# A hybrid decoder layer: query squares added in pairs of half-heads, queries split from an SBUF copy, keys transposed once, adding transfers in another order

## The chip, the core and the metric

The kernel runs on one NeuronCore of one Trainium2 chip. A core has a matrix engine (TensorE, here PE, with its weight loads shown as PEld), three elementwise engines (VectorE or DVE, ScalarE or ACT, GpSimd or POOL) and a queue engine (SyncE or SP). Each works through its own instruction list in order and waits on semaphores for the others. SBUF is the working memory of 128 partitions, PSUM the memory that PE writes. The metric is the device time of one execution in microseconds, as the median of several runs.

## The reference

The layer takes `x` of 512 tokens by 1024 channels in float32. Only the attention part is touched in what it computes; the MLP keeps its arithmetic.

```
u = rms_norm(x, norm_mix_g)                       # 512 x 1024
proj = u @ w_in                                   # queries, keys, values, GLU pair, two gates
q = rms_norm(q, q_norm_g) * HEAD_DIM ** -0.5      # 16 heads of 64
k = rms_norm(k, k_norm_g)                         # 4 heads of 64
attn = sliding_window_attention(q, k, v, sinks, rel_bias) @ w_attn_o   # blocks of 128, window 128
conv = conformer_conv(glu_in, ...)                # 31 taps per channel, layer norm, silu, projection
x = x + (sigmoid(gate_attn) * attn + sigmoid(gate_conv) * conv) @ w_out
x = x + square(relu(rms_norm(x, norm_mlp_g) @ w_ff1)) @ w_ff2          # 1024 -> 4096 -> 1024
```

`rms_norm` of the queries needs, for every token and head, the mean of 64 squares.

## The kernel before

**Precision.** PE multiplies in a reduced float32 form, `fp32r`. To keep float32 accuracy every operand is split into a high part (a cast to `fp32r`) and a low part (the value less its high part), and a product is three matmuls: high by high, high by low, low by high. A weight piece of 128x1024 therefore costs ACT a cast (`split_hi`, L469) and POOL a subtraction (`split_lo`, L474) before PE can use it. Transposes are matmuls against an identity.

**Order.** Nothing is scheduled automatically. The code registers closures with `at(position, function, ...)`; at the end they are sorted by position (L1536) and run, and each engine's list is what they issue in that order. In the first part one position is one step of a projection tile: six matmuls of 128x512 (two of the eight chunks of 128 channels, three products each), and a tile of 128 output columns is four steps. The tiles follow as `h0 h1 q0 h2 q1 h3 h4 h5 q2 h6 h7 q3`, where `h` is a pair of GLU tiles (gate `ps_g`, value `ps_a`) and `q` a query group of two tiles (`ps_q`), then the gates `ps_ta` and `ps_tc`. Between the steps stand the attention units, one for each of 4 groups g and 4 token blocks t, at 42 + 6 (4 g + t): scores (`sp`, L712 and L713), scale (L720, ACT), maximum (L727, DVE), exponentials (L735, ACT), division (L744, POOL), transpose of the probabilities (`ptp`, L752), their split (L755 ACT, L759 DVE) and the product with the values (`op`, L767 and L769). DVE runs the taps of the convolution (L826) through this whole stage, ACT and POOL a few of them (L817, L818).

**Keys.** The keys of all groups lie token by token in `kraw`. `k_hi` (ACT) and `k_lo` (POOL) write their high and low parts, each twice side by side so that both halves of the 128 partitions hold them; `k_stage` (L405) transposes both parts, four 128x128 blocks per part and group, and ACT copies each result out of PSUM (L409).

**Queries.** A query tile holds two heads of 64 rows. When PE has finished it, ACT takes the high part of each head from PSUM (`q_hi`, L547) and the squares of the whole tile (`q_square`, L550), and DVE the low part of each head (`q_lo`, L554). After a group's second tile ACT and POOL split all squares into high and low parts (L566, L569). At `QSUM` = 8.08 positions after the group, `q_sums` (L571) adds over the 64 rows on PE: for each of 2 tiles, 4 token blocks and 2 parts one matmul with the squares as weights and the two columns of `pair` as moving operand, 16 per group into `qms`. ACT adds epsilon (L578) and POOL takes the inverse root (L580), which scales the scores.

**MLP.** It is cut into four parts of 1024 hidden units, each with two phases (`w_ff1`, then `w_ff2`), and each phase is a product of 2x2 block matrices with seven products instead of eight, in Strassen's manner (numbers 1 to 7). A product takes 4 positions, half a weight block at a time: ACT makes the high piece (`pieceh`, L1168), DVE the low one (`piecel`, L1171), 24 or 48 matmuls use them. Sums of weight blocks are made by DVE (`block_sum`, L1161) or in flight: `fetch_add` (L1145) issues on POOL's queue a transfer that adds a block of HBM to one in SBUF. In the second phases the order is 1, 7, 6, 2, 5, 4, 3. The transfers that add for product 5 go into product 1's block once both its pieces are read, those for product 6 into product 7's block, those for product 4 into that block again after product 6. Each is issued 0.9 positions after its half's high piece.

Of the kernel before, what the change touches and what calls it, by code (L numbers as in the profile page):

```python
# [8 lines left out]
F32 = mybir.dt.float32  # L9
F32R = mybir.dt.float32r  # L10
# [7 lines left out]
P = 128  # L18
# [24 lines left out]
QSUM = 8.08  # L43
# [10 lines left out]
def tile_hybrid_block(  # L54
# [197 lines left out]
    pair = sm.tile([P, 16], F32R, name="pair", tag="ss16")[:, 0:2]  # L252
# [142 lines left out]
    def k_hi(j):  # L395
        if j == 0:
            k2["h"] = att.tile([P, 16, 2, HD], F32R, name="k2h", tag="qs")
            k2["l"] = gates[:, 0].rearrange("p k c -> p (k c)").rearrange("p (t a d) -> p t a d", a=2, d=HD)
        se.copy(k2["h"][:, :, j, :], k3)

    def k_lo(j):
        ge.tensor_tensor(out=k2["l"][:, :, j, :], in0=k3, in1=k2["h"][:, :, j, :].bitcast(F32), op=ALU.subtract)

    def k_stage(nm, dst, g):
        tp = ps1.tile([P, S], F32R, name=f"ktp_{nm}{g}", tag="tr")  # L405
        for t in range(NT):
            pe.transpose(tp[:, t * P:(t + 1) * P],
                         k2[nm][:, t * NG + g].rearrange("p a d -> p (a d)"), ident_r)
        se.copy(dst[:, g, :], tp.bitcast(F32))  # L409
# [4 lines left out]
    for j in range(2):  # L414
        at(4.5 + j, k_hi, j)
        at(6.5 + 2 * j, k_lo, j)
    for g in range(NG):
        at(9.5 + 2 * g, k_stage, "h", kTh, g)
        at(18.5 + 2 * g, k_stage, "l", kTl, g)
# [117 lines left out]
    def q_open(g):  # L537
        qTs[g] = qTt[:, (1 + g) % 2].rearrange("p k c -> p (k c)").rearrange("p (h t q) -> p h t q", t=NT, q=P)
        state["sq", g] = att.tile([P, 2, NT, P], F32, name=f"sq_{g}", tag="qs")

    def q_from(ps, a):
        rows = slice(a * HD, (a + 1) * HD)
        return rows, ps[rows].rearrange("p (t q) -> p t q", q=P)[:, :, ::-1]

    def q_hi(ps, g, j, a):
        rows, src = q_from(ps, a)
        se.copy(qTs[g][rows, 2 * j + a], src)  # L547

    def q_square(ps, g, j):
        se.activation(state["sq", g][:, j], ps.rearrange("p (t q) -> p t q", q=P)[:, :, ::-1], AF.Square)  # L550

    def q_lo(ps, g, j, a):
        rows, src = q_from(ps, a)
        ve.tensor_tensor(out=qTs[g][(1 - a) * HD:(2 - a) * HD, 2 * j + a], in0=src,  # L554
                         in1=qTs[g][rows, 2 * j + a].bitcast(F32), op=ALU.subtract)

    def pair_of():
# [1025 lines left out]
```

## Time and profile before

| what | value |
|---|---|
| median of 3 runs | 753.25 us (753.12 to 754.34) |
| profiled execution | 754.29 us, of which the profile's span 752.5 us |
| PE busy | 745.1 us, 99% of the span |
| DVE, ACT, POOL busy | 614.1, 463.8, 264.8 us |
| granted PE clock | 1.00 in every stage |
| bytes moved | 97.96 MB, 130 GB/s on average |

The stages by the profile's clock: keys and values of the input projection to 32 us, then the projection tiles with the attention units and the convolution to about 300 us, the three output projections to about 440 us, and the MLP to the end. A row of the groups reads: line, engine, operation, output <- inputs, shapes, count | busy us, mean ns of one | idle time of the engine just before, and what ended it. A row of the timeline reads: start us, duration us, engine, line, operation, and in square brackets the idle time before it with what ended it. Matmuls overlap in the pipeline, so the price of a matmul in a row of them is the distance between starts, not the duration. An f32 matmul that isn't a transpose appears as two rows.

### The profile page before, as it was taken

What the parts mean: (1) busy time and instruction counts of PE and PEld (TensorE: products, weight loads), DVE (VectorE), ACT (ScalarE), POOL (GpSimd) and SP (SyncE); (2) the same over time, 40 slices, a digit from 0 to 9 for tenths busy, and PEclk for the clock granted to TensorE, in tenths of its full rate; (3) what the DMA queues carried; (4) which work ended last, traced back from release to release, by engine and by line L of the source; (5) the groups of instructions that cost most, each with busy time, mean ns of one, the idle gap of its engine ahead of it and who ended that gap; (6) DMA issues with size and microseconds to landing.
All of it is one profiled execution on the core that took longest, in us unless ns stands there. A gap on an engine that the chain in (4) does not pass through costs nothing.

```text
span 752.5 us, 11081 instructions
## 1 busy us (share of the span) xinstructions
PE 745.1 (99%) x4146; PEld 644.7 (86%) x4146; DVE 614.1 (82%) x934; ACT 463.8 (62%) x755; POOL 264.8 (35%) x212
## 2 busy tenths in 40 slices
PE   9999999999999999999999999999999999999998
PEld 7888888888888888888888899879997899889976
DVE  7948988989988988878347679899779977998786
ACT  7647467868877766348225468763765467546752
POOL 0466777666676565433530002210121012101210
PEclk9999999999999999999999999999999999999999
DMA  8531122232114131613329107972697359834772
GB/s 320 197 104 37 56 73 96 85 112 84 57 59 139 56 112 57 223 57 112 112 71 345 35 26 144 247 197 85 155 220 191 106 132 230 196 116 122 171 156 112
DMA packets 64901, 97.96 MB, mean 130 GB/s; under 512 B 3104, under 2 KB 34384, under 8 KB 64848
## 3 DMA queue, kind: packets, MB, share of 16 engines
q1 hardware_dynamic: 55600, 79.44, 31.3%
q0 software_dynamic: 9248, 17.83, 13.5%
q8 instruction: 32, 0.52, 0.3%
q14 instruction: 21, 0.17, 0.1%
HBM read 95.13 MB, written 2.12 MB: 129 GB/s over the span
## 4 chain that ended last, share of the span: by engine, by line
PE 81%; DMA 6%; issue 5%; DVE 5%; ACT 2%; POOL 1%; DVEq 0%; POOLq 0%; ACTq 0%
PE ps_z L1205 9%; DMA block<-in_w_ff_dram 6%; PE ps_x L1200 5%; PE ps_y L1205 4%; PE ps_kv L1401 3%; PE ps_y L1200 3%; PE ps_x L1205 3%; PE ps_g L506 2%; PE ps_a L506 2%; PE ps_g L508 2%; PE ps_g L507 2%; PE ps_a L508 2%; PE ps_a L507 2%; PE ps_tc L508 2%; PE ps_tc L507 2%
## 5 line engine op out<-in xcount | busy, mean ns | idle before, releaser
L1168 ACT CAST pieceh<-block 128x1024 fp32r<-128x1024 f32 x112 | 115.8, 1049 | 76.7 <-DVE block L1161 22.9
L1171 DVE TENSOR_TENSOR piecel<-block,pieceh 128x1024 fp32r<-128x1024 f32 x112 | 135.6, 1219 | 28.5 <-ACT pieceh L1168 28.3
L826 DVE SCALAR_TENSOR_TENSOR cv<-h,wcol,cv 128x512 f32<-128x512 f32 x208 | 146.2, 746 | 0.7
L1147 POOL DMA_DIRECT2D block<-in_w_ff_dram x34 | 41.4, 1259 | 291.7 <-DVE piecel L1171 145.8
L1200 PE MATMUL ps_x<-xSh,pieceh 128*128 128x256 f32 x192 | 53.0, 276 | 0.0
L1200 PE MATMUL ps_x<-xSl,pieceh 128*128 128x256 f32 x192 | 53.0, 276 | 0.0
L1200 PE MATMUL ps_x<-xSh,piecel 128*128 128x256 f32 x192 | 53.0, 276 | 0.0
L1205 PE MATMUL ps_z<-piecel,aSh 128*128 128x512 f32 (+1 forms) x98 | 38.4, 392 | 1.5 <-DVE piecel L1171 1.5
L1205 PE MATMUL ps_z<-pieceh,aSh 128*128 128x512 f32 (+1 forms) x98 | 37.9, 386 | 0.5 <-ACT pieceh L1168 0.5
L1205 PE MATMUL ps_z<-pieceh,aSl 128*128 128x512 f32 (+1 forms) x98 | 37.7, 385 | 0.0
L1161 DVE TENSOR_TENSOR block<-block,block 128x1024 f32<-128x1024 f32 x30 | 36.5, 1221 | 0.8 <-DMA block<-in_w_ff_dram 0.4
L1200 PEld LDWEIGHTS ps_x<-xSh,pieceh 128*128 128x128 f32 x192 | 36.0, 188 | 0.0
L1200 PEld LDWEIGHTS ps_x<-xSl,pieceh 128*128 128x128 f32 x192 | 36.0, 188 | 0.0
L1200 PEld LDWEIGHTS ps_x<-xSh,piecel 128*128 128x128 f32 x192 | 36.0, 188 | 0.0
L735 ACT ACTIVATE s<-s,negm 128x257 f32<-128x257 f32 (+1 forms) x64 | 30.3, 477 | 7.2 <-DVE negm L727 7.0
L818 POOL TENSOR_TENSOR side<-side,tap 128x512 f32<-128x512 f32 x24 | 31.0, 1292 | 10.0 <-ACT tap L817 10.0
L1239 ACT CAST aSh<-c 128x1024 fp32r<-128x1024 f32 x16 | 16.8, 1053 | 23.5 <-DVE c L1253 11.1
L727 DVE CUSTOM_DVE_ANT_0 s<-sp,bias,vecs 128x256 f32<-128x256 f32 (+1 forms) x64 | 26.0, 445 | 6.4 <-ACT sp L720 6.1
L744 POOL TENSOR_TENSOR s<-s,r 128x1024 f32<-128x1024 f32 (+1 forms) x16 | 26.9, 1681 | 10.9 <-DVE r L739 10.8
L720 ACT ACTIVATE sp<-sp,y_q 128x256 f32<-128x256 f32 (+1 forms) x64 | 25.8, 420 | 7.0 <-PE sp L713 6.0
L474 POOL TENSOR_TENSOR wl_g<-raw_g,wh_g 128x1024 fp32r<-128x1024 f32 x8 | 19.3, 2409 | 30.3 <-ACT wh_g L469 30.3
L474 POOL TENSOR_TENSOR wl_wo<-raw_wo,wh_wo 128x1024 fp32r<-128x1024 f32 x8 | 19.8, 2480 | 25.2 <-ACT wh_wo L469 25.2
(335 smaller groups left out, 2495.2 us busy)
## 6 DMA issues: line engine op xcount, KB each, us to landing
block<-in_w_ff_dram SPq DMA_DIRECT2D x64, 512.0 KB, 5.9
block<-in_w_ff_dram POOLq DMA_DIRECT2D x34, 512.0 KB, 8.5
raw_g<-in_w_in_dram SPq DMA_DIRECT2D x8, 512.0 KB, 4.3
raw_a<-in_w_in_dram SPq DMA_DIRECT2D x8, 512.0 KB, 4.4
raw_q<-in_w_in_dram SPq DMA_DIRECT2D x8, 512.0 KB, 3.8
raw_ta<-in_w_in_dram SPq DMA_DIRECT2D x8, 512.0 KB, 3.8
raw_tc<-in_w_in_dram SPq DMA_DIRECT2D x8, 512.0 KB, 3.9
raw_wo<-in_w_attn_o_dram SPq DMA_DIRECT2D x8, 512.0 KB, 3.8
```

The costliest lines, as they stand in the source:

```text
L474: eng.tensor_tensor(out=lo, in0=raw, in1=hi.bitcast(F32), op=ALU.subtract)
L507: pe.matmul(ps, wh[:, k, :], al(k), start=False, stop=False)
L508: pe.matmul(ps, wl[:, k, :], ah(k), start=False, stop=(k == KD - 1))
L735: se.activation(s4[:, h, lo:2 * P + 1], s4[:, h, lo:2 * P + 1], AF.Exp, bias=negm[:, h:h + 1], scale=-1.0, accum_out=l4[:, h:h + 1])
L818: ge.tensor_tensor(out=side[ct], in0=side[ct], in1=tap, op=ALU.add)
L826: ve.scalar_tensor_tensor(out=cps[ct], in0=src, scalar=w, in1=cps[ct], op0=ALU.mult, op1=ALU.add)
L1147: ge.dma_start(tl["raw"][buf][:, ks, :], block(ph, i, j)[:, ks, :], accum_op=ALU.add)
L1161: ve.tensor_tensor(out=o, in0=a, in1=b, op=ALU.add)
L1168: se.copy(piece("h", n), tl["raw"][buf][:, 2 * h:2 * h + 2, :])
L1171: ve.tensor_tensor(out=piece("l", n), in0=tl["raw"][buf][:, 2 * h:2 * h + 2, :], in1=piece("h", n).bitcast(F32), op=ALU.subtract)
L1200: pe.matmul(o, b[:, c, w], a[:, k, :], start=(first and c + q + i == 0), stop=(k == 3 and i == 2), skip_group_check=True)
L1205: pe.matmul(acc[:, cols], a[:, k, w], b[:, c, cols], start=(first and c + i == 0), stop=(k == 3 and i == 2), skip_group_check=True)
```

## The change

It has four parts.

1. **Sums of squares.** The square of a tile is replaced by `q_square` per head and half-head: each call writes the squares of 32 rows to the 32 partitions of that head in one tile `sq`, first 32 channels in one half of it, last 32 in the other. POOL adds the two halves (`q_square_sum`, 128x512). `q_sums` is then one plain f32 matmul per token block, 4 per group, against `pick` with four columns. The split of the squares (L566, L569) and `pair` are gone. `QSUM` becomes 10.08 for the first two groups and 9.42 for the others.
2. **Queries.** DVE copies the finished tile from PSUM to `qraw` (`q_keep`); the high parts, the squares (ACT) and the low parts (now POOL) read that copy, at later positions (`HI`, `SQ`, `LO`).
3. **Keys.** ACT writes the keys themselves twice side by side in f32 (`k_twice`), PE transposes them once as f32, ACT casts the result to the high part, and DVE subtracts to the low part.
4. **Adding transfers.** In the MLP's second phases the two transfers into product 1's block move from about 5 and 3 positions before the phase to 1.0 and 1.05 after its start.

```diff
-QSUM = 8.08
+QSUM = (10.08, 10.08, 9.42, 9.42)
+HI, SQ, LO = (6.6, 4.6), (7.0, 8.6), (6.8, 4.8)
...
-    def k_hi(j):
...
-        se.copy(k2["h"][:, :, j, :], k3)
-    def k_lo(j):
-        ge.tensor_tensor(out=k2["l"][:, :, j, :], in0=k3, in1=k2["h"][:, :, j, :].bitcast(F32), op=ALU.subtract)
-    def k_stage(nm, dst, g):
...
+    def k_twice(j):
+        if j == 0:
+            k2["d"] = att.tile([P, 16, 2, HD], F32, name="k2d", tag="qs")
+        se.copy(k2["d"][:, :, j, :], k3)
+    def k_stage(g):
+        tp = k2["t", g] = ps1.tile([P, S], F32, name=f"ktp_{g}", tag="tr")
         for t in range(NT):
+            pe.transpose(tp[:, t * P:(t + 1) * P], k2["d"][:, t * NG + g].rearrange("p a d -> p (a d)"), ident)
+    def k_hi(g):
+        se.copy(kTh[:, g, :], k2["t", g])
+    def k_lo(g):
+        ve.tensor_tensor(out=kTl[:, g, :], in0=k2["t", g], in1=kTh[:, g, :].bitcast(F32), op=ALU.subtract)
...
     for g in range(NG):
-        at(9.5 + 2 * g, k_stage, "h", kTh, g)
-        at(18.5 + 2 * g, k_stage, "l", kTl, g)
+        at(9.5 + 2 * g, k_stage, g)
+        at(9.6 + 2 * g, k_hi, g)
+        at(9.8 + 2 * g, k_lo, g)
...
+    def q_keep(ps, g, j):
+        ve.tensor_copy(state["raw", g][:, j], ps.rearrange("p (t q) -> p t q", q=P)[:, :, ::-1])
+    def q_hi(g, j, a):
         rows = slice(a * HD, (a + 1) * HD)
+        se.copy(qTs[g][rows, 2 * j + a], state["raw", g][rows, j])
+    def q_square(g, j, a):
+        h = 2 * j + a
+        for half in range(2):
+            rows = slice(a * HD + 32 * half, a * HD + 32 * half + 32)
+            se.activation(state["sq", g][32 * h:32 * h + 32, half], state["raw", g][rows, j], AF.Square)
+    def q_lo(g, j, a):
+        rows = slice(a * HD, (a + 1) * HD)
+        ge.tensor_tensor(out=qTs[g][(1 - a) * HD:(2 - a) * HD, 2 * j + a], in0=state["raw", g][rows, j],
                          in1=qTs[g][rows, 2 * j + a].bitcast(F32), op=ALU.subtract)
...
+    def q_square_sum(g):
+        sq = state["sq", g]
+        ge.tensor_tensor(out=sq[:, 0], in0=sq[:, 0], in1=sq[:, 1], op=ALU.add)
     def q_sums(g):
...
-        for j in range(2):
-            for t in range(NT):
-                for n in "hl":
-                    pe.matmul(ms_ps[:, t, 2 * j:2 * j + 2], state["sq" + n, g][:, j, t, :], pair, start=n == "h", stop=n == "l")
+        for t in range(NT):
+            pe.matmul(ms_ps[:, t, :], state["sq", g][:, 0, t, :], pick, start=True, stop=True)
...
+            at(b + 4.2, lambda cell=cell, j=j: q_keep(cell["ps"], g, j))
             for a in range(2):
+                at(b + HI[j] + 0.1 * a, q_hi, g, j, a)
+                at(b + SQ[j] + 0.6 * a, q_square, g, j, a)
+                at(b + LO[j] + 0.4 * a, q_lo, g, j, a)
             b += 4
-        at(b + 0.9, q_square_hi, g)
-        at(b + 1.2, q_square_lo, g)
-        at(b + QSUM, q_sums, g)
-        at(b + QSUM + 0.4, q_root, g)
+        at(b + 6.6, q_square_sum, g)
+        at(b + QSUM[g], q_sums, g)
+        at(b + QSUM[g] + 0.4, q_root, g)
...
                 elif prod == 1:
-                    at(d, fetch_add, ph, h11, 0, 1, h)
+                    at(m + 1.0 + 0.05 * h, fetch_add, ph, h11, 0, 1, h)
```

Line numbers shift by three after the change, since it makes the file three lines shorter from the query part on.

Three places of the lists, of before and of the change. First, ACT at the third query group, around the second pair of exponentials (`s_...` with `negm`) of the attention unit next to the group's end; `h_...` with `cv` is a finished convolution tile, `tap` one of its taps, `wh_...` a high weight piece, `ms_q` the epsilon step after the sums. Before:

```order
L469 CAST wh_a_1_1636<-raw_a_1309 128x1024
L837 ACTIVATE h_782<-cv_927,wcol 128x512
L735 ACTIVATE s_1575,l_1577<-s_1575,negm_1576 128x257 x2
L817 ACTIVATE tap_3_1666<-h_1016,wcol 128x512
L703 COPY s_1684<-vecs 128x4
L578 ACTIVATE ms_q_1723<-qms_1706,eps_ln 128x16
```

and with the change:

```order
L470 CAST wh_a_1_1604<-raw_a_1276 128x1024
L834 ACTIVATE h_762<-cv_897,wcol 128x512
L732 ACTIVATE s_1543,l_1545<-s_1543,negm_1544 128x257 x2
L554 ACTIVATE sq_1438<-qraw_1437 32x512 x4
L814 ACTIVATE tap_3_1639<-h_990,wcol 128x512
L700 COPY s_1657<-vecs 128x4
```

The four squares of the group's second tile, which stood one piece ahead of `wh_g` as a single row of 128x512, now follow the exponentials, and the epsilon step has moved behind six more rows.

Second, POOL at the same group (`wl_...` a low weight piece, `s_...<-s_...,r_...` the division of the probabilities, `qTt` a low query part). Before:

```order
L474 TENSOR_TENSOR wl_g_1_1541<-raw_g_1180,wh_g_1_1540 128x1024
L569 TENSOR_TENSOR sql_1551<-sq_1470,sqh_1550 128x1024
L527 MEMSET h_1633 128x30
L474 TENSOR_TENSOR wl_a_1_1637<-raw_a_1309,wh_a_1_1636 128x1024
L744 TENSOR_TENSOR s_1575<-s_1575,r_1578 128x4x256
L818 TENSOR_TENSOR side_1192<-side_1192,tap_3_1666 128x512
```

and with the change:

```order
L475 TENSOR_TENSOR wl_g_1_1511<-raw_g_1147,wh_g_1_1510 128x1024
L558 TENSOR_TENSOR qTt<-qraw_1437,qTt 64x512 x2
L528 MEMSET h_1601 128x30
L475 TENSOR_TENSOR wl_a_1_1605<-raw_a_1276,wh_a_1_1604 128x1024
L741 TENSOR_TENSOR s_1543<-s_1543,r_1546 128x4x256
L568 TENSOR_TENSOR sq_1438<-sq_1438 128x512
L815 TENSOR_TENSOR side_1159<-side_1159,tap_3_1639 128x512
```

The low squares have gone, two low queries stand in their place, and the add of the two square halves stands behind the next low weight piece and a division.

Third, POOL's queue of transfers at the first two phases of the MLP: `block0` holds product 1's weights in the first second phase, `block3` product 7's. Before:

```order
L1147 DMA block1_3844<-in_w_ff1_dram 128x2x512 x2
L1147 DMA block3_3954<-in_w_ff2_dram 128x2x512 x2
L1147 DMA block0_3843<-in_w_ff2_dram 128x2x512 x2
L1147 DMA block3_3954<-in_w_ff2_dram 128x2x512 x4
L1147 DMA block1_3844<-in_w_ff2_dram 128x2x512 x2
```

and with the change:

```order
L1144 DMA block1_3799<-in_w_ff1_dram 128x2x512 x2
L1144 DMA block3_3909<-in_w_ff2_dram 128x2x512 x4
L1144 DMA block0_3798<-in_w_ff2_dram 128x2x512 x2
L1144 DMA block3_3909<-in_w_ff2_dram 128x2x512 x2
L1144 DMA block1_3799<-in_w_ff2_dram 128x2x512 x2
```

The two transfers into `block0` have moved behind the first two of the four into `block3`, those of product 7; the last two of the four, product 6's, stay behind both.

More of the change, by code (lines that the diff above doesn't have):

```diff
@@ L251, in tile_hybrid_block @@
     ssk = sm.tile([P, 16], F32, name="ssk", tag="ss16")
-    pair = sm.tile([P, 16], F32R, name="pair", tag="ss16")[:, 0:2]
+    pick = sm.tile([P, 16], F32, name="pick", tag="ss16")[:, 0:GRP]
     gates = gpool.tile([P, 2, KD, 256], F32R, name="gates", tag="gate")
@@ L414, in tile_hybrid_block @@
     for j in range(2):
-        at(4.5 + j, k_hi, j)
-        at(6.5 + 2 * j, k_lo, j)
+        at(4.5 + j, k_twice, j)
     for g in range(NG):
-        at(9.5 + 2 * g, k_stage, "h", kTh, g)
-        at(18.5 + 2 * g, k_stage, "l", kTl, g)
+        at(9.5 + 2 * g, k_stage, g)
+        at(9.6 + 2 * g, k_hi, g)
+        at(9.8 + 2 * g, k_lo, g)
     T_SHAPE = [P, KD, P]
@@ L538, in q_open @@
         qTs[g] = qTt[:, (1 + g) % 2].rearrange("p k c -> p (k c)").rearrange("p (h t q) -> p h t q", t=NT, q=P)
+        state["raw", g] = att.tile([P, 2, NT, P], F32, name=f"qraw_{g}", tag="qraw", bufs=2)
         state["sq", g] = att.tile([P, 2, NT, P], F32, name=f"sq_{g}", tag="qs")
-    def q_from(ps, a):
+    def q_keep(ps, g, j):
+        ve.tensor_copy(state["raw", g][:, j], ps.rearrange("p (t q) -> p t q", q=P)[:, :, ::-1])
+    def q_hi(g, j, a):
         rows = slice(a * HD, (a + 1) * HD)
-        return rows, ps[rows].rearrange("p (t q) -> p t q", q=P)[:, :, ::-1]
@@ L545, in q_hi @@
[L545 to L554, printed above, removed]
-                         in1=qTs[g][rows, 2 * j + a].bitcast(F32), op=ALU.subtract)
-    def pair_of():
-        low = eps_ln[:, 4:6]
-        ge.memset(low, 0.0)
-        for a in range(2):
-            ge.memset(low[a * HD:(a + 1) * HD, a:a + 1], 1.0 / HD)
-        ge.tensor_copy(pair, low)
@@ L564, in q_square_hi @@
-    def q_square_hi(g):
-        state["sqh", g], state["sql", g] = [att.tile([P, 2, NT, P], F32R, name=f"sq{n}_{g}", tag="qraw", bufs=2) for n in "hl"]
-        se.copy(state["sqh", g], state["sq", g])
-    def q_square_lo(g):
-        ge.tensor_tensor(out=state["sql", g], in0=state["sq", g], in1=state["sqh", g].bitcast(F32), op=ALU.subtract)
+        se.copy(qTs[g][rows, 2 * j + a], state["raw", g][rows, j])
[4 more added lines that the diff above has]
+            se.activation(state["sq", g][32 * h:32 * h + 32, half], state["raw", g][rows, j], AF.Square)
@@ new lines, in q_lo, with pick_of @@
+    def q_lo(g, j, a):
+        rows = slice(a * HD, (a + 1) * HD)
+        ge.tensor_tensor(out=qTs[g][(1 - a) * HD:(2 - a) * HD, 2 * j + a], in0=state["raw", g][rows, j],
+                         in1=qTs[g][rows, 2 * j + a].bitcast(F32), op=ALU.subtract)
+    def pick_of():
+        ge.memset(pick, 0.0)
+        for h in range(GRP):
+            ge.memset(pick[32 * h:32 * h + 32, h:h + 1], 1.0 / HD)
+    def q_square_sum(g):
+        sq = state["sq", g]
+        ge.tensor_tensor(out=sq[:, 0], in0=sq[:, 0], in1=sq[:, 1], op=ALU.add)
@@ L596, in tile_hybrid_block @@
     b = 0
-    at(0.3, pair_of)
+    at(0.3, pick_of)
     glu_chunks = {}
```

9 lines of the change are left out of this document (removed).

## The prediction

> **What bounds the kernel now.** I read the page first, then the table of busy time by stage, then who waited for whom on TensorE (PE).
>
> ```profile
> span 752.5 us, 11081 instructions
> PE 745.1 (99%) x4146; PEld 644.7 (86%) x4146; DVE 614.1 (82%) x934; ACT 463.8 (62%) x755; POOL 264.8 (35%) x212
> ```
> ```profile
> 140.00:180.00 40.00, 40.00 (x210) 33.90 (x209) 35.12 (x79) 31.67 (x77) 24.85 (x27) 1.00 0.20 65
> ```
> ```profile
> PE ps_z L1205 <- DVE piecel L1171: 1.5, 3, 0.8
> ...
> PE ps_z L1205 <- ACT pieceh L1168: 0.5, 1, 0.5
> PE op L769 <- DVE pTl L759: 0.3, 1, 0.3
> ```
>
> PE is busy in 745.1 of 752.5 us. The stage row (columns: PE, weight loads, VectorE (DVE), ScalarE (ACT), GpSimd (POOL), granted clock) says the same for the attention stage: PE 40.00 of 40.00 at full clock, while the others have 5 to 15 us free. So the kernel ends when PE's list ends. An instruction taken off PE's list is worth its place in that list, and other engines matter only where PE must wait for them. PE's waits that the change can reach are the first two rows: 1.5 + 0.5 = 2.0 us, all in front of `ps_z` in the second halves of the MLP's phases.
>
> **The sums of the query squares.** The third group's sums on the timeline (start, duration; 16 rows in all from the first to the last), and the nearest row to the new form, a plain f32 sum against a narrow operand:
>
> ```profile
> 163.05 0.17 PE L576 MATMUL qms<-pair,sqh 128*128 128x2 f32 x1
> ...
> 164.64 0.25 PE L576 MATMUL qms<-pair,sql 128*128 128x2 f32 x1
> 164.75 0.48 PE L506 MATMUL ps_g<-uTh,wh_g 128*128 128x512 f32 x1
> ```
> ```profile
> 326.61 1.05 PE L932 MATMUL var_ps<-ones,vsum 128*128 128x1 f32 x8
> 327.52 0.48 PE L506 MATMUL ps_wo<-aTh,wh_wo 128*128 128x512 f32 x1
> ```
>
> Today 16 rows hold PE from 163.05 to 164.75, 1.70 us, though each moves two columns: a row costs 0.11 us whatever its width. The change issues 4 f32 matmuls per group. The variance sum is the same form: 4 calls appear as 8 rows, and the next matmul starts 0.91 us later. The new operand has 4 columns, the old one 1; both are far below the 128 that today's rows of like price move, so I take 0.91. The saving is 0.79 a group, 3.2 us for four. Bounds: if the wider operand made every row twice as dear, 0; if the calls ran as one row each, 5.0.
>
> [...]
>
> **The keys.** Today every group is transposed twice, high and low parts, four transposes each:
>
> ```profile
> 59.77 0.46 PE L407 MATMUL ktp_l<-ident_r,gates 128*128 128x128 f32 x4
> 60.06 0.47 PE L506 MATMUL ps_q<-uTh,wh_q 128*128 128x512 f32 x1
> 60.37 0.39 PE L507 MATMUL ps_q<-uTl,wh_q 128*128 128x512 f32 x1
> ```
> ```profile
> 117.37 0.60 PE L752 MATMUL ptp<-ident,s 128*128 128x128 f32 x4
> 117.72 0.48 PE L506 MATMUL ps_g<-uTh,wh_g 128*128 128x512 f32 x1
> 118.04 0.39 PE L507 MATMUL ps_g<-uTl,wh_g 128*128 128x512 f32 x1
> ```
>
> A burst costs 60.37 - 59.77 = 0.60, less the 0.23 of the matmul inside it, 0.37 us. Plain f32 transposes, which the probabilities already use, cost 118.04 - 117.37 = 0.67, less 0.23, 0.44. Four bursts go (1.5) and four become f32 (+0.3): 1.2 us off PE.
>
> **The adding transfers.** In the second phase of each pair the product order is 1, 7, 6, 2, 5, 4, 3, and product 6 needs the sum that product 7's transfers add. POOL's issues, ACT's high pieces, PE's first two matmuls of product 6 and a whole product on the chain, and the time to landing (first, second, fourth transfer), in the first such phase:
>
> ```profile
> 475.62 1.21 POOL L1147 DMA_DIRECT2D block<-in_w_ff_dram  x1 [14.09 <-DVE piecel L1171]
> 477.95 2.44 POOL L1147 DMA_DIRECT2D block<-in_w_ff_dram  x2 [1.12 <-DVE piecel L1171]
> 482.07 1.22 POOL L1147 DMA_DIRECT2D block<-in_w_ff_dram  x1 [1.68 <-issue]
> ```
> ```profile
> 488.32 2.00 ACT L1168 CAST pieceh<-block 128x1024 fp32r<-128x1024 f32 x2 [3.72 <-DMA block<-in_w_ff_dram]
> 490.64 1.05 ACT L1168 CAST pieceh<-block 128x1024 fp32r<-128x1024 f32 x1 [0.33 <-DMA block<-in_w_ff_dram]
> ```
> ```profile
> 489.42 0.51 PE L1205 MATMUL ps_z<-pieceh,aSh 128*128 128x512 f32 x1 [0.50 <-ACT pieceh L1168]
> 490.68 0.50 PE L1205 MATMUL ps_z<-piecel,aSh 128*128 128x512 f32 x1 [0.75 <-DVE piecel L1171]
> ...
> 496.34 5.44 PE ps_x L1205 x24
> ```
> ```profile
> DMA to landing us min/median/max: 6.1/6.1/6.1
> ...
> DMA to landing us min/median/max: 6.9/6.9/6.9
> ...
> DMA to landing us min/median/max: 8.5/8.5/8.5
> ```
>
> The first two issues are product 1's halves, the third (at about 479.1) and fourth are product 7's. The third lands just before 488.32, some 9.1 us after its issue; the first in the line needs 6.1, the second 6.9. PE waits 0.50 us for the high and 0.75 for the low piece. With product 7's halves first, the issue is hardly earlier, since it waits for its own low piece, but it lands like today's first: 479.1 + 6.1 = 485.2, 3 us sooner, more than any of the four waits (2.0 together). I take 2.0. What is late next: product 7's second half, 482.07 + 6.9 = 489.0; ACT's 1.05 and the 1.26 from the high to the low piece (489.42 to 490.68) make it ready at 491.3. Product 6 would then start at 488.9 and want it half a product, 2.7 us, later, at 491.6. That just holds. Product 1's halves go out after 483.3, at today's worst land near 492.5, and are wanted by product 5, two products of 5.44 after product 6's start, at 499.8. They hold nothing but product 6's two transfers behind them on POOL. Bounds: 0 to 2.0.
>
> **What moves to other engines.** Prices of the nearest rows:
>
> ```profile
> L818 POOL TENSOR_TENSOR side<-side,tap 128x512 f32<-128x512 f32 x24 | 31.0, 1292 | 10.0 <-ACT tap L817 10.0
> L569 POOL TENSOR_TENSOR sql<-sq,sqh 128x1024 fp32r<-128x1024 f32 x4 | 9.6, 2404 | 0.0
> L554 DVE TENSOR_TENSOR qTt<-ps_q,qTt 64x512 fp32r<-64x512 f32 x16 | 11.0, 689 | 3.7 <-ACT sq L550 3.4
> L759 DVE TENSOR_TENSOR pTl<-ptp,pTh 128x512 fp32r<-128x512 f32 x28 | 19.0, 684 | 7.9 <-ACT pTh L755 7.9
> L550 ACT ACTIVATE sq<-ps_q 128x512 f32<-128x512 f32 x8 | 4.8, 599 | 0.1
> L1065 ACT ACTIVATE fsq<-x x8: 632/633/643, 413.1 to 439.9; 128x512 f32<-128x512 f32 x8
> ACT ms_q L578 <- PE qms L576: 13.9, 4, 6.2
> ```
>
> DVE pays by columns and not by rows (64 rows 689 ns, 128 rows 684). It loses 16 low parts (11.0 us) and gains 8 copies and 4 key low parts (12 x 0.68 = 8.2): 2.8 us lighter. ACT loses 8 squares (4.8), 4 casts of 128x1024 (4.2 at the 1.05 above) and 4 key copies (2.4, priced like the squares), and gains 32 squares of 32 rows; if they too pay by columns, 0.63 each, 20.3 us: 8.9 us heavier. No row shows one of 32 rows; a price by rows would be a quarter, so 5 to 20. I take 20, as DVE's rows teach. POOL loses 4 low squares and, at the same shape, 2 low keys (6 x 2.40 = 14.4) and gains 16 low queries and 4 adds of 512 columns (20 x 1.29 = 25.8): 11.4 us heavier, over a stage in which the row above has it free 15 us in 40. So the totals hide. What can fail is order: the squares of a group's second half now stand behind the second pair of exponentials, POOL adds them after that, and PE's sums wait for the add. In the third group (161 to 165 us) and the fourth:
>
> ```profile
> 161.12 0.20 ACT L735 ACTIVATION_READ_ACCUMULATOR s<-s,negm 128x1 f32 x1
> 161.21 0.72 ACT L817 ACTIVATE tap<-h,wcol 128x512 f32<-128x512 f32 x1
> 164.93 0.27 ACT L578 ACTIVATE ms_q<-qms,eps_ln 128x16 f32<-128x16 f32 x1 [2.91 <-PE qms L576]
> ...
> 206.44 0.20 ACT L703 COPY s<-vecs 128x4 f32<-128x4 f32 x1 [0.59 <-PE ptp L752]
> 210.40 0.27 ACT L578 ACTIVATE ms_q<-qms,eps_ln 128x16 f32<-128x16 f32 x1 [3.76 <-PE qms L576]
> ```
>
> The exponentials end at 161.3 on today's clock. PE reaches the new place of the sums, one step (1.4) and a value product (0.5) after 163.05, at 165.0. By then PE is ahead by 1.2 (keys) and 2 x 0.8 (two earlier sums): 162.2. If ACT follows with the same 2.8 and 0.3 of its own more work, the exponentials end at 158.8, four squares at 161.3, the add at 162.6, and hand-over makes 162.7: PE waits 0.5 us. In the fourth group ACT idles 0.59 + 3.76 = 4.35 there, 1.4 more than in the third, and the sums move back as far, so the 0.5 turns into a margin of about 0.9. Over all four groups ACT idles 13.9 us ahead of the sums, 6.2 at most in one, against 4 x 2.5 of late squares. I take 0.6 given back in all; bounds 0 and about 4.2 (rival one).
>
> **The sum:** -3.2 - 1.2 - 2.0 + 0.6 = -5.8 us. The profiled execution took 754.29 us, its 752.5 span and 1.8 around it; it becomes 748.5. It lies 1.04 above the median of the runs, 753.25; on that the forecast is 747.5 us. Its own range, with give-back 0 to 2, is 746.5 to 749.2.
>
> **Rivals.** One: *the sums wait in most groups.* If the chain through squares and POOL's add runs 2 to 3 us later than worked out (0.72 a square as for taps, DVE late with the copy), the third group waits 3 and the fourth, with its 0.9 of margin, up to 1.2 more once the third's wait has moved PE back: 4.2 given back, 751.1. For: the third group's margin is already negative. Against: DVE is lighter and ACT idles 2.91 there now.
>
> Two: *the reorder gains nothing,* because other queues and not the earlier adds stretch the landing: 747.5 + 2.0 = 749.5. For: the fourth transfer takes 8.5 as well. Against: the first in line takes 6.1 beside the same traffic.
>
> Three: *the f32 sums cost as many rows as now:* 747.5 + 3.2 = 750.7. Against: the variance row.
>
> Four, the slower side: *POOL cannot carry the low queries in time.* They stand ahead of the low weight pieces in its queue, which PE takes next; it decides once POOL's backlog passes the lead of a piece. If all of POOL's 11.4 us came through, 747.5 + 11.4 = 758.9. Against: its free time.
>
> **How the numbers follow.** Forecast 0.66, sums waiting 0.16, reorder idle 0.10, f32 rows 0.04, POOL late 0.04. The range runs from full gain on a low median, 746.3, over the three rivals that still gain, to 751.1. A measurement of this kernel tells 0.2%, 1.5 us, from no change: faster means below 751.7. Half of the reach of rival one lies near that line: faster 0.90, same 0.05, slower 0.05.
>
> **What would show it.** Right: 32 rows of sums in four bursts of 0.9 us, 16 key transposes in four of 0.44, no wait of `ps_z` in the MLP's second phases, product 7's first half landing in 6 to 7 us, and PE waits before the sums of under 1 us in total. Wrong: PE waits before the sums, released by POOL's add, in three groups; or `ps_z` waiting at product 6 or 5; or PE waiting for low weight pieces between 60 and 220 us.

## The result and the profile after

The changed kernel takes 749.86 us (median of 6 executions, 749.20 to 750.71), the kernel before 753.28 in the same comparison: a ratio of 0.9947 (95% interval 0.9929 to 0.9964), 3.4 us less by the medians. The forecast was 747.5 us, 5.8 less. The profiled execution took 750.46, of which the span is 748.7.

The busy times of the changed kernel, and then its table of waits on PE (engine, tile and line, who releases it: us in total, times, longest):

```profile
PE 740.2 (99%) x4098; PEld 641.1 (86%) x4098; DVE 610.7 (82%) x930; ACT 475.5 (64%) x771; POOL 276.3 (37%) x227
```
```profile
PE op L764 <- ACT pTh L752: 1.2, 1, 1.2
...
PE qms L573 <- POOL sq L568: 0.7, 1, 0.7
...
PE op L766 <- DVE pTl L756: 0.5, 2, 0.3
```

Every wait of `ps_z` in the MLP is gone. In its place PE waits at a value product (`op`) and at one group's sums (`qms`). To see what each part was worth, the same matmul is looked up in both traces, and the difference of its starts is how far PE is ahead:

| place in PE's list | before, us | after, us | ahead, us |
|---|---|---|---|
| after the last key transposes | 69.47 | 68.25 | 1.2 |
| after the second group's sums | 110.54 | 107.28 | 3.3 |
| one step before the third group's value product | 164.75 | 160.09 | 4.7 |
| after that product and the sums | 166.79 | 164.76 | 2.0 |
| nine matmuls later | 168.89 | 168.49 | 0.4 |
| after the fourth group's sums | 212.26 | 211.83 | 0.4 |
| first MLP phase with adding transfers, end of its waits | 493.88 | 491.62 | 2.3 |
| the same in the second | 571.01 | 567.93 | 3.1 |
| the same in the last | 724.50 | 720.56 | 3.9 |

Of the 4.7 us, 0.8 are the third group's own sums, which the changed kernel still has in front of it there. Nearly all of the rest is lost in the third and fourth groups, and the MLP gives more than forecast. Two errors of the forecast stand against each other. The third group's value product on PE's timeline, first before:

```profile
166.22 0.39 PE L767 MATMUL op<-pTh,vv 128*128 128x512 f32 x1
166.45 0.50 PE L769 MATMUL op<-pTl,vv 128*128 128x512 f32 x1
```

and with the change, from the matmul in front of it to the first ones behind the sums:

```profile
161.25 0.39 PE L509 MATMUL ps_g<-uTh,wl_g 128*128 128x512 f32 x1
162.89 0.51 PE L764 MATMUL op<-pTh,vv 128*128 128x512 f32 x1 [1.25 <-ACT pTh L752]
163.62 0.50 PE L766 MATMUL op<-pTl,vv 128*128 128x512 f32 x1 [0.22 <-DVE pTl L756]
163.95 0.95 PE L573 MATMUL qms<-pick,sq 128*128 128x4 f32 x8
164.76 0.78 PE L507 MATMUL ps_g<-uTh,wh_g 128*128 128x512 f32 x1
165.34 0.63 PE L508 MATMUL ps_g<-uTl,wh_g 128*128 128x512 f32 x1
165.76 0.63 PE L509 MATMUL ps_g<-uTh,wl_g 128*128 128x512 f32 x1
```

PE waits 1.25 us for the high and 0.22 for the low probabilities; against the kernel before this costs 1.33 and 0.49 (the ends of matmuls are modelled, 0.39 us after a start, while the next may start after 0.23, so a wait costs more than its bracket says). The sums behind it find their operands ready. Then something appears that the kernel before did not have: from 164.76 on a 128x512 matmul takes 0.43 us from start to start instead of 0.23. The busy time by stretches (length, PE, weight loads, DVE, ACT, POOL, granted clock, DMA share, GB/s) says why:

```profile
164.00:166.00 2.00, 2.00 (x12) 1.81 (x11) 1.47 (x6) 1.93 (x6) 2.00 (x2) 0.69 0.11 38
166.00:168.00 2.00, 2.00 (x6) 1.52 (x6) 1.26 (x6) 1.99 (x8) 1.58 (x6) 0.50 0.00 0
168.00:170.00 2.00, 2.00 (x10) 1.66 (x9) 1.99 (x4) 1.44 (x6) 1.43 (x8) 0.95 0.00 0
```

The granted clock is 0.50 for (1.00 - 0.69) x 2 / 0.5 + 2.0 + (1.00 - 0.95) x 2 / 0.5 = 3.4 us. PE is "busy" all that time and loses another 1.6 us (2.0 to 0.4 in the table). This also splits the six executions in two: 749.20, 749.23 and 749.30 at a mean granted clock of 1.000, 750.41, 750.46 and 750.71 at 0.998. The profiled one is of the second kind.

What held the probabilities, on ACT's timeline:

```profile
158.97 2.55 ACT L554 ACTIVATE sq<-qraw 32x512 f32<-32x512 f32 x4
161.55 0.72 ACT L814 ACTIVATE tap<-h,wcol 128x512 f32<-128x512 f32 x1
...
162.26 0.57 ACT L752 CAST pTh<-ptp 128x512 fp32r<-128x512 f32 x1
```

The four late squares and a tap stand in front of the cast. In the fourth group the wait is at the sums, as forecast for the third; POOL's and PE's rows:

```profile
208.34 1.29 POOL L815 TENSOR_TENSOR side<-side,tap 128x512 f32<-128x512 f32 x1
209.59 1.27 POOL L568 TENSOR_TENSOR sq<-sq 128x512 f32<-128x512 f32 x1
```
```profile
210.92 1.05 PE L573 MATMUL qms<-pick,sq 128*128 128x4 f32 x8 [0.70 <-POOL sq L568]
```

The squares ended at 207.5 there; the add stood two more microseconds behind the division and a tap in POOL's queue. Last, the first MLP phase with adding transfers: POOL's issues, the time to landing of the first, ACT's high pieces, and PE at product 6:

```profile
478.40 1.21 POOL L1144 DMA_DIRECT2D block<-in_w_ff_dram  x1 [17.18 <-DVE piecel L1168]
480.77 2.44 POOL L1144 DMA_DIRECT2D block<-in_w_ff_dram  x2 [1.16 <-DVE piecel L1168]
```
```profile
DMA to landing us min/median/max: 6.4/6.4/6.4
```
```profile
484.85 2.14 ACT L1165 CAST pieceh<-block 128x1024 fp32r<-128x1024 f32 x2 [0.88 <-DMA block<-in_w_ff_dram]
488.87 1.05 ACT L1165 CAST pieceh<-block 128x1024 fp32r<-128x1024 f32 x1 [1.88 <-DMA block<-in_w_ff_dram]
```
```profile
488.45 0.39 PE L1202 MATMUL ps_z<-pieceh,aSh 128*128 128x512 f32 x1
```

Product 6 starts 3.6 us after its first high piece was begun. The second half's high piece is done at 489.9 and PE wants it at 491.17.

### The profile page after: what moved, and what is told of

It reads as the page before. It is cut to its first block, busy times and chain, and to the rows that moved or that the text cites. A ratio compares the mean times of both kernels' runs of the same rounds, so it can differ in the third digit from the quotient of the medians.

```text
span 748.7 us, 11014 instructions
## 1 busy us (share of the span) xinstructions
PE 740.2 (99%) x4098; PEld 641.1 (86%) x4098; DVE 610.7 (82%) x930; ACT 475.5 (64%) x771; POOL 276.3 (37%) x227
## 4 chain that ended last, share of the span: by engine, by line
PE 90%; ACT 4%; DVE 2%; issue 1%; DMA 1%; POOL 1%; SPq 0%; DVEq 0%; ACTq 0%; POOLq 0%
PE ps_x L1197 12%; PE ps_z L1202 12%; PE ps_y L1202 6%; PE ps_y L1197 6%; PE ps_z L1197 3%; PE ps_x L1202 3%; PE ps_kv L1398 3%; PE ps_tc L509 2%; PE ps_tc L508 2%; PE ps_wo L193 2%; PE ps_wo L192 2%; PE ps_tc L507 2%; PE ps_wc L509 2%; PE ps_wc L508 2%; PE ps_wo L191 2%; PE ps_wc L507 2%
## 5 line engine op out<-in xcount | busy, mean ns | idle before, releaser
L756 DVE TENSOR_TENSOR pTl<-ptp,pTh 128x512 fp32r<-128x512 f32 x28 | 19.1, 687 | 12.4 <-ACT pTh L752 12.3
```

## The experiments

Two theories at the start. A: a local queue, the four squares in front of the cast on ACT. B: ACT and POOL, with some 11 us more to do each, are too full, and any repair only moves the wait. Beside the experiments the kernel before had medians of 754.4 to 755.0 and scattered more (752.5 to 756.8) than in the first comparison. By the record experiments 1 to 4, 5 to 8 and 9 to 12 ran on three different chips, each beside runs of the kernel before. So times are compared by their ratios to it, which carry about 0.16% either way, and where that is too coarse the traces decide.

**1. Squares and add early in the third group.**

```diff
-                at(b + SQ[j] + 0.6 * a, q_square, g, j, a)
+                at(b + (7.25 + 0.05 * a if (g, j) == (2, 1) else SQ[j] + 0.6 * a), q_square, g, j, a)
...
-        at(b + 6.6, q_square_sum, g)
+        at(b + (6.6, 6.6, 4.9, 6.6)[g], q_square_sum, g)
```

> The changed kernel, but in the third group the four squares of the second half stand on ScalarE ahead of the exponentials instead of behind them, and GpSimd adds them ahead of the norm of the probabilities. Theory A (a local queue): the value product waited because its high probabilities stood behind those four squares; PE idled 1.25 and 0.22 us there, which cost 1.82 us against the kernel before, and the half clock behind it another 1.49. Here the value product and the sums start without a wait, near 161.6, the granted clock stays 1.00 over the stretch, the span is 3.3 us shorter than the profiled 748.7, that is 745.4, and the median 747.2 (749.2 less 1.82 for the executions without the clock's dip, 750.5 less 3.3 for those with it). Rival B (ScalarE and GpSimd are too full, each has some 11 us more to do): the wait only moves to another place between 150 and 215 us, and the span stays within 0.5 us of 748.7.

Measured: 749.17 us (748.59 to 749.92), ratio 0.9928 (0.9913 to 0.9944), profiled span 748.0. PE's and then DVE's timeline:

```profile
160.89 0.39 PE L764 MATMUL op<-pTh,vv 128*128 128x512 f32 x1
162.77 0.50 PE L766 MATMUL op<-pTl,vv 128*128 128x512 f32 x1 [1.48 <-DVE pTl L756]
```
```profile
158.73 0.18 DVE L736 RECIPROCAL r<-l 128x4 f32<-128x4 f32 x1 [1.62 <-ACT s L732]
158.82 0.72 DVE L821 TENSOR_SCALAR cv<-h,wcol 128x512 f32<-128x512 f32 x1
159.46 2.06 DVE L823 SCALAR_TENSOR_TENSOR cv<-h,wcol,cv 128x512 f32<-128x512 f32 x3
161.43 0.68 DVE L533 SCALAR_TENSOR_TENSOR h<-h,ps_a 128x512 f32<-128x512 f32 x1
162.03 0.69 DVE L756 TENSOR_TENSOR pTl<-ptp,pTh 128x512 fp32r<-128x512 f32 x1
```

Theory A falls for the most part. The high probabilities are no longer late, yet PE waits 1.48 us for the low ones. DVE's reciprocal waits for the exponentials of the next attention unit, and 3.2 us of taps and a GLU product stand between it and the low part. The clock still drops in three of six executions (0.998). With the squares out of the way about 1.6 us are lost in place of 1.82, so their late place was worth 0.2 to 0.3 us.

**2. Squares early, the add left late.** Only the first of the two edits above.

> As the run before it, but GpSimd's add stays behind the norm of the probabilities. Theory A: the value product no longer waits; the norm on GpSimd ends at 161.7 as now, the add at 163.0, PE reaches the sums at 162.1 and waits 0.9 to 1.0 us there: about 1.1 us lost in the third group in place of 1.82 plus 1.49. Whether so short a wait brings the half clock is open: span 746.5 without it, 748.0 with it. A rival, that GpSimd's add was the limit all along and the squares do not matter: the wait at the sums is as long as the one at the value product was, 1.25 us or more, and nothing is gained.

Measured: 749.09 us (748.38 to 750.41), ratio 0.9929 (0.9913 to 0.9946), span 747.7; the same table of waits as in experiment 1, 1.5 us for `pTl` and none at the third group's sums. Neither expectation holds. The wait for the low probabilities is so long that the add is done when PE gets to the sums. As long as that wait stands, the place of the add in the third group is of no account.

**3. Kernel before, adding transfers alone.** `at(m + 1.0 + 0.05 * h, fetch_add, ph, h11, 0, 1, h)` in place of `at(d, ...)`.

> The kernel before with only the adding transfers reordered. Reading A (how far every matmul after the wait came sooner): 3.5 us less, 749.8 us, in steps of about 1.8, 0.8 and 0.9 in the three phases. Reading B (the recorded idle time, as predicted): 2.0 us less, 751.3. Reading C (the gain in the MLP needs the earlier arrival from the first half of the kernel): less than 1 us, 752.3 or more.

Measured: 750.93 us (750.51 to 751.06), ratio 0.9950 (0.9934 to 0.9966), 2.6 to 5.0 us less than the kernel before on that chip; span 749.1, no wait of `ps_z`. Against the trace of before its matmuls come 0.1 us later at 10 us and 3.4 earlier at the end: 3.5 us, reading A. The absolute time lies between the readings, since the kernel before took 1.7 us more in this comparison than in the first; ratio and trace both exclude 2.0.

**4. Kernel before, query part alone.** All of the query part, keys and transfers as before.

> The kernel before with only the query part of the change (copies, 32 squares of 32 rows, added pairs, four sums a group); keys and adding transfers as before. The sums save about 3.5 us. Theory A, if ScalarE's and VectorE's chain into the third group runs on its own: PE comes 1.2 us later to the third group than with the keys, so the wait at the value product is 0.6 us and not 1.8, there is no half clock, and the fourth group gives back 0.75: 3.5 - 0.6 - 0.75 = 2.1 us less, 751.1. If that chain follows PE: all of 4.1 is given back, and the time is 753.3 to 753.9, no gain from this part at all. By the prediction as it stood (0.6 given back): 750.7.

Measured: 754.73 us (752.96 to 758.24, 12 executions), ratio 1.0005 (0.9988 to 1.0022). This part alone gains nothing, as the second reading of theory A has it. Its waits on PE, and the clock after the third group:

```profile
PE qms L573 <- POOL sq L568: 1.3, 2, 0.7
PE op L764 <- ACT pTh L752: 1.3, 1, 1.3
```
```profile
166.00:168.00 2.00, 2.00 (x10) 1.91 (x10) 1.47 (x6) 1.93 (x5) 2.00 (x2) 0.50 0.28 97
168.00:170.00 2.00, 2.00 (x5) 1.61 (x6) 1.32 (x5) 1.99 (x8) 1.61 (x5) 0.50 0.00 0
170.00:172.00 2.00, 2.00 (x6) 1.52 (x6) 1.93 (x4) 1.03 (x5) 1.49 (x7) 0.50 0.00 0
172.00:174.00 2.00, 2.00 (x9) 1.59 (x8) 1.97 (x5) 0.82 (x2) 1.83 (x4) 0.79 0.00 0
```

The wait at `op` is as long as in the whole change, though PE is 1.2 us later without the keys: the chain of scores, exponentials and probabilities follows PE, so an earlier PE does not by itself outrun it. At the sums PE waits in the first and the fourth group, not in the third. The half clock lasts 6 + (1.00 - 0.79) x 2 / 0.5 = 6.8 us in this profile; six of the twelve executions have a mean clock of 0.996 or less. It begins at 166.0, ahead of the sums, which start at 166.26; so in this profile the sums did not bring it.

So what had outrun the chain? For the most part the order of PE's list. The sums, 1.70 us, stood between the scores and the value product; the change puts them behind the product. That is theory A2, tested next from both sides.

**5. Value product and sums later.**

```diff
-QSUM = (10.08, 10.08, 9.42, 9.42)
+QSUM = (10.08, 10.08, 11.02, 10.42)
...
-            at(u0 + 15.4, value, g, t)
+            at(u0 + 15.4 + 1.6 * ((g, t) == (1, 0)), value, g, t)
```

and the same 1.6 on `value_low` and `value_sum`.

> The changed kernel with the value product in the third group and the sums behind it moved later in TensorE's list, behind nine matmuls of 0.23 us that have their inputs, and the sums of the fourth group later by one step (six matmuls, 1.4 us). Theory A2, formed from the first experiment: the wait is no matter of the squares alone. The scores of the next quarter, their scaling, maxima and exponentials, VectorE's reciprocal that waits for these, and the 3.5 us of taps behind it in VectorE's queue, end in the low probabilities at about 163.6; TensorE comes there too early because the sums, 1.70 us that stood in front of the value product, now stand behind it. Nine matmuls (2.1 us) in front cover it: no wait in the third group, none for GpSimd's add in the fourth, clock 1.00 in every execution, span about 744.6 (748.7 less 1.82, 1.49 and 0.75), median 746.6. Rival B (the engines are too full): the wait comes back at the next value product or sums, and the time stays within 0.5 of the changed kernel's 749.2 to 750.5.

Measured: 747.29 us (747.14 to 747.60), ratio 0.9908 (0.9893 to 0.9923), span 745.6, clock 0.999 or more in all six. The waits at `op` in the third group and at the fourth group's sums are gone. Here 12 matmuls were put in front, not nine. One new wait, PE's and DVE's rows:

```profile
170.28 0.63 PE L749 MATMUL ptp<-ident,s 128*128 128x128 f32 x4 [1.14 <-DVE attnT L777]
```
```profile
169.28 0.85 DVE L777 TENSOR_TENSOR attnT<-op,osb 64x256 f32<-64x256 f32 x2
```

The value product, now late, is also copied out late, and the next transposes wait for its buffer. So theory A2 holds for the first wait, with a grain of B: 1.1 us moved on.

**6. Sums later, nothing else.** `QSUM = (10.08, 10.08, 11.42, 11.42)`.

> The changed kernel with only the sums of the third and fourth groups two steps later (12 matmuls, 2.7 us); the value products stay. The wait at the value product in the third group stays (1.82 us), the wait for GpSimd's add in the fourth (0.75) goes. What it tells is the clock: in the changed kernel the half clock begins at the end of 1.47 us of idle time and 0.8 us of sums with four columns. If idle time alone brings it, half of the executions still show a clock under 1.00 (749.8), the others 748.5. If the sums beside it are needed (an array that moves four columns counts as idle), no execution shows it: 748.5 in all.

Measured: 748.07 us (747.36 to 749.66), ratio 0.9920 (0.9903 to 0.9936). The wait at `op` is 1.29 and 0.23 us, the fourth group's is gone. One execution of six shows a clock under 0.999, the profiled one, with 3.4 us at 0.50. So 1.5 us of idle time was followed by the half clock with no sums beside it; whether the sums make it likelier, one in six against three in six cannot tell.

**7. Kernel before, its sums moved behind the value product.** `QSUM` 9.42 for the third and fourth groups, the 16 fp32r matmuls kept.

> The kernel before, its sums of squares in the third and fourth groups moved behind the value product as in the change, nothing else. Theory A2: TensorE comes to the value product 1.70 us sooner, near 164.5; the exponentials of the next quarter end at 161.3 and VectorE's queue behind them takes 3.5 us and 0.7 for the low probabilities, which end near 165.5: a wait of about 0.8 us released by VectorE, and 1.0 to 1.4 us in all over both groups, 754.3 to 754.7. If the squares on ScalarE were the cause, nothing here waits: 753.3.

Measured: 754.09 us (752.75 to 759.50, 12 executions), ratio 1.0005 (0.9987 to 1.0023): the medians do not show it. The trace does, PE's and DVE's rows:

```profile
164.44 0.39 PE L767 MATMUL op<-pTh,vv 128*128 128x512 f32 x1
165.40 0.50 PE L769 MATMUL op<-pTl,vv 128*128 128x512 f32 x1 [0.58 <-DVE pTl L759]
```
```profile
161.37 0.18 DVE L739 RECIPROCAL r<-l 128x4 f32<-128x4 f32 x1 [1.60 <-ACT s L735]
...
164.67 0.68 DVE L759 TENSOR_TENSOR pTl<-ptp,pTh 128x512 fp32r<-128x512 f32 x1
```

PE comes at 164.44, as worked out, and waits until the low part ends at 165.35, with no square on ACT changed. The two starts lie 0.96 us apart in place of 0.23, so the wait costs 0.73. In this execution the half clock follows, from 167.24 on, at the end of the sums. Nothing is lost in the fourth group, so the upper part of the expectation was too high.

**8. Kernel before, keys alone.**

> The kernel before with only the keys' part of the change. Four bursts of transposes of 0.37 us go, four become 0.44: 1.2 us less, 752.0. If the matmuls between had hidden them: 753.3. Nothing else moves, since the third group keeps its sums in front of the value product.

Measured: 752.28 us (751.39 to 753.55, 12 executions), ratio 0.9970 (0.9957 to 0.9982), 1.4 to 3.2 us less. In the trace PE is 1.24 us ahead after the four bursts (0.09 to 1.33), and 0.75 at the end: `ps_z` waits five times in the MLP, 2.2 us in all, where the kernel before waits four times, 2.0. That the comparison shows more than the trace may come from the kernel before, which had a mean clock of 0.998 or less in 5 of its 23 executions beside these, and this kernel in none of 12; that is not shown.

**9. Both repairs.** Edits of experiment 1, `QSUM = (10.08, 10.08, 10.32, 10.42)`, and

```diff
+            at(u0 + 15.4 + 0.9 * ((g, t) == (1, 0)), value, g, t)
...
+            at(u0 + (15.93 if ahead else 16.1) + 0.4 * ((g, t) == (1, 0)), value_low, g, t)
+            at(u0 + (15.94 if ahead else 16.4) + 0.4 * ((g, t) == (1, 0)), value_sum, g, t)
```

> The changed kernel with three things at once in the third group: squares and add early as in the first experiment, the value product and the sums six matmuls (1.4 us) later, and the product's evacuation only as much later as it must be; in the fourth group the sums one step later. In the fifth experiment the wait was gone at the value product, but 1.14 us came back 5 us later, where the next transposes waited for a buffer that VectorE's sum of the late value product had not yet freed. By the theory of a fixed chain the low probabilities end near 162.7 (first experiment), TensorE reaches them at 163.2, and the evacuation stands ahead of the second pair of exponentials: no wait of either kind, 1.4 us less than the fifth experiment, span near 744.2, median 745.9. If the wait only moves on again: 747.3 or more.

Measured: 746.55 us (746.16 to 747.20), ratio 0.9896 (0.9880 to 0.9912), span 745.0, clock 0.999 or more in all. Its whole table of waits on PE:

```profile
PE warm L209 <- PEq L1562: 0.8, 1, 0.8
PE ps_kv L1398 <- DVE roots L1410: 0.7, 1, 0.7
PE op L766 <- DVE pTl L756: 0.3, 1, 0.3
PE ps_kv L1398 <- ACT gates L330: 0.2, 1, 0.2
```

No wait for the sums is left, and none for the buffer. It is the fastest kernel of the study, 0.6 us above what was expected.

**10. Idle time alone, longer.** Experiment 6 with `at(b + 5.3, q_square, g, 1, 1)` once more for `g == 2`.

> The kernel of the sixth experiment (sums moved away from the value product) with two of the third group's squares done twice, 1.27 us more on ScalarE ahead of the high probabilities. TensorE's idle time at the value product becomes 2.6 to 2.8 us in place of 1.5, with nothing narrow beside it. If idle time alone brings the half clock, and the more the longer, most of the executions show a clock of 0.998 or less and 3.41 us at 0.50; those without are near 749.4, those with it near 750.9. If the narrow sums were what brought it: a clock of 1.00 in nearly all, 749.4.

Measured: 749.78 us (749.05 to 751.06), ratio 0.9939 (0.9925 to 0.9954). Three of six executions at 0.998 (750.35 to 751.06), three at 0.999 or 1.000 (749.05 to 749.21). PE's row and the stretch behind it (the edit makes the file two lines longer):

```profile
164.50 0.49 PE L766 MATMUL op<-pTh,vv 128*128 128x512 f32 x1 [2.57 <-ACT pTh L754]
```
```profile
165.70:169.10 3.40, 3.40 (x10) 2.65 (x9) 2.50 (x10) 3.31 (x10) 2.35 (x2) 0.50 0.00 0
```

With 2.8 us of idle time and no narrow sums beside it the profile has the half clock, and half of the executions have the lower mean clock.

**11. Narrow matmuls alone.** Experiment 5 with the third group's four sums issued three times over.

> The kernel of the fifth experiment, in which nothing waits at the value product, with the sums of the third group done three times over: 2.4 us of matmuls that move four columns each, back to back, no idle time beside them. If such matmuls count as idle for the clock, some executions show a stretch of 3.41 us at 0.50 right behind them (time near 750.5); if only idle time counts, none does: 747.3 plus 1.6, 748.9 in all.

Measured: 747.67 us (747.19 to 750.97), ratio 0.9916 (0.9899 to 0.9934).

```profile
164.84 2.74 PE L573 MATMUL qms<-pick,sq 128*128 128x4 f32 x24
```

Five executions lie at 747.2 to 747.8 with a clock of 1.000, one at 750.97 with 0.994. That one is no proof, since no profile caught where its clock fell. Of the 1.6 us of added work only 0.4 appears: the sums fill the time in which experiment 5 waited for the buffer.

**12. The changed kernel again.**

> The changed kernel unaltered, on the chip that ran the experiments, so that they can be set beside it. If the steps read so far hold, its executions fall in two groups as on the first chip, near 749.2 at a clock of 1.00 and near 750.5 at 0.998, and its ratio to the kernel before lies 0.4 to 0.5% above that of the kernel with both fixes (0.9896): 0.994 to 0.995. If the fixes gained nothing of their own and the chips only differ, its ratio is 0.990 too, 747 us.

Measured: 749.89 us (749.19 to 751.94), ratio 0.9941 (0.9927 to 0.9955). Two executions at 749.19 and 749.35 (1.000 and 0.999), four between 749.81 and 751.94 (0.998 to 0.995). The profiled one had 6.8 us of half clock behind the same 1.3 us wait. The record gives the same chip for this experiment and the ninth, and the kernel before took the same beside both (754.53 and 754.45). The interval of the ratio and that of experiment 9 do not meet: the repairs gain 3.3 us by the medians.

The halved clock by kernel; a dip is an execution with a mean clock of 0.998 or less, and the PE time is that of the profile around the third group's value product:

| kernel | idle, us | narrow sums beside it, us | dips |
|---|---|---|---|
| after, and experiment 12 | 1.5 | 0.8 | 3 of 6, 4 of 6 |
| experiments 1, 2 | 1.5 | 0.8 | 3 of 6 each |
| 4 | 1.5 | 0.8 | 6 of 12 |
| 7 | 0.6 | 1.7 | 4 of 12 |
| 6 | 1.5 | none | 1 of 6 |
| 10 | 2.8 | none | 3 of 6 |
| 11 | none | 2.7 | 1 of 6 |
| 5 | 1.1, five us later | none | 0 of 6 |
| 9 | under 0.2 | 0.8 | 0 of 5 |

Experiments 3 and 8, which keep the sums in front of the value product, show no dip in 6 and 12 executions. The kernel before, too, dips in 13 of its 62 executions beside the experiments. Where, no profile shows; it stays open.

## Why the prediction was right and where it was wrong

The time fell within the range and the direction was right, but by terms that were off in both directions. That it fell within is partly luck: the give-back that was missed, 3.5 us, would alone have brought 747.5 to 751.0, just under the upper end of 751.1, and 1.5 us more than forecast from the adding transfers pulled it back:

| term | forecast, us | measured, us |
|---|---|---|
| keys | -1.2 | -1.2 |
| sums | -3.2 | -3.5 |
| adding transfers | -2.0 | -3.5 |
| given back | +0.6 | +4.1: third group 1.8, half clock 1.6, fourth group 0.7 |
| sum | -5.8 | -4.1; the last matmul ends 4.0 earlier, the span is 3.8 shorter |

**Keys: right.** Four bursts, at the price of f32 transposes: 46.59 - 45.92 = 0.67 from the first one's start to the second matmul behind it, less 0.23, is 0.44 us, and experiment 8 has PE 1.24 us ahead behind all four.

**Sums: right.** A burst of eight rows took 0.80 to 0.81 us three times and 0.91 once, where 0.91 was taken from the variance sum. As many rows as before, 16 a group, would have given 750.7 us; the trace again has two rows a call, and 32 for the four groups. The 0.11 us a row "whatever its width" holds for the narrow rows of the traces (0.11 for 1 and 2 columns before, 0.10 for 4 now, 0.11 for the f32 transposes of 128) and not for 512 columns, where 0.23 lie between starts.

**Adding transfers: right mechanism, size too small.** The first half landed in 6.4 us, ahead of need, and the second "just holds": its low piece ends at 491.2 and PE wants it at 491.39. But 2.0 was the sum of the recorded waits. From matmul to matmul, PE's lead grows by 0.66, 1.04 and some 0.25 in the first phase, and by about 0.55 and 0.25 in each of two others: 3.5. A recorded wait leaves out the stretch between the earliest possible next start and the modelled end of the matmul before. For the wait of 0.75 that the prediction quotes this is 0.51 - 0.23 = 0.28, and the two starts beside it, 1.26 apart, give the full 1.03. The three steps of 0.25 were not listed as waits at all. The upper bound of 2.0 was therefore none.

**Other engines: totals about right.** ACT rose by 11.7 (8.9 forecast), POOL by 11.5 (11.4), DVE fell by 3.4 (2.8). Squares of 32 rows cost what was taken, 629 ns where 128 rows of 512 columns took 632 before (L1065), and so did POOL's low queries, 1289 ns for 64 rows where a tap of 128 took 1292 (L818):

```profile
L554 ACT ACTIVATE sq<-qraw 32x512 f32<-32x512 f32 x32 | 20.1, 629 | 0.4
L558 POOL TENSOR_TENSOR qTt<-qraw,qTt 64x512 fp32r<-64x512 f32 x16 | 20.6, 1289 | 4.7 <-ACT qTt L548 3.5
```

**The give-back: the step that failed.** The prediction followed squares, add and sums, and found PE at the new place of the sums at 162.2, "one step (1.4) and a value product (0.5) after" the old one, less its lead. It walked PE through that value product without asking whether its operands would be there. They were not: with 1.70 us of sums moved from its front to its back, PE came to it that much sooner. Experiment 7 puts the move alone at 0.7 us. Experiment 1, with the squares out of the way, still loses about 1.6, so another 0.9 has a second source, and it is not the earlier PE. From the first score of the next unit to DVE's reciprocal the chain takes 9.8 us in the kernel before, in experiment 7 and in experiment 8, where PE comes 1.2 us earlier; it takes 10.6 in the changed kernel and in experiment 4, and 10.9 in experiment 1. What differs is ACT's list. In the changed kernel four squares, a weight piece and two high queries fill it from 144.05 to 148.85 in front of an earlier unit's high probabilities, and DVE waits 3.18 us for these; in the kernel before it has other work there and does not wait. ACT's and DVE's rows of the changed kernel:

```profile
144.05 2.56 ACT L554 ACTIVATE sq<-qraw 32x512 f32<-32x512 f32 x4
...
147.59 1.26 ACT L548 CAST qTt<-qraw 64x512 fp32r<-64x512 f32 x2
148.87 0.59 ACT L752 CAST pTh<-ptp 128x512 fp32r<-128x512 f32 x1
```
```profile
149.49 0.69 DVE L756 TENSOR_TENSOR pTl<-ptp,pTh 128x512 fp32r<-128x512 f32 x1 [3.18 <-ACT pTh L752]
```

So part of rival B of the experiments holds: ACT's new work makes the chain longer. It is read from the traces; no run moved these instructions alone. In experiment 1 four more squares stand in front of the exponentials, which may be its further 0.3. The late squares add the last 0.2 to 0.3, to 1.82. In the fourth group the forecast margin of 0.9 became a wait of 0.7: it counted ACT's idle time and not POOL's queue, where a division and a tap stood ahead of the add. The fifth and ninth experiments take both away. The half clock was on no list.

**Rivals.** The first (sums wait in most groups, 4.2 given back, 751.1) came nearest in size, with another mechanism: only one group's sums waited. The second and third are refuted by experiment 3 and by the eight rows. The fourth, POOL late with low pieces, did not happen: no wait of PE on a low weight piece appears.

**What would show it.** 32 rows in four bursts, 16 key transposes, no `ps_z` wait in the second phases, a landing in 6 to 7 us: all seen. PE's waits before the sums of under 1 us: 0.7, seen, and yet it was the wrong place to look, since the larger wait stood one instruction earlier.

## What to carry to other kernels

When an instruction is moved behind another on the bounding engine, the one it passes comes sooner by the moved one's length (here 1.70 us): follow the operands of that one too, through every queue (here a reciprocal and 3.2 us of other work on DVE), and ask whether the change has lengthened their chain (here by 0.8 us). What a removed wait is worth is read from starts, as the distance between the two starts less the usual one, not from the recorded idle time (here 1.03 us where 0.75 was recorded). And a short wait on PE can cost more than itself: here three of six executions show a lower mean clock and took 1.3 us longer, the profiled one of them with 0.50 for 3.4 us behind 1.5 us of waiting.

## What the runs showed of the hardware that was not expected

After 1.5 us of idle PE time, with 0.8 us of four-column sums beside it or without, the granted clock fell to 0.50 for 3.4 us (after, experiments 1, 2 and 6) or twice that, 6.8 us (experiments 4 and 12); in experiment 7 it fell for 3.4 us with 0.6 us idle beside 1.7 us of two-column sums. It did so in some executions and not in others of the same kernel, and cost 1.3 us by the two groups of the changed kernel's executions (749.2 against 750.5). The 1.14 us of experiment 5 brought it in none of six.

It does not begin at the end of the wait. In the trace of the changed kernel the granted clock is 1.00 up to 164.77 and 0.50 from there to 168.19, 1.1 us after the last wait at the value product ended at 163.62. In experiment 4 it falls at 166.0, 0.2 us after that wait's end at 165.82, and in experiment 7 at 167.24, 1.8 us after its end at 165.40. What sets the time of the fall, and why other executions of the same kernel are spared, is not shown: no profile caught one of them. In the two profiles with 6.8 us, 1.6 and 0.7 us of the narrow sums fall into the first 3.4 us at half clock, in the others at most 0.4; whether that is why it went on, two profiles do not show.
